# A two-block model on one core: x loaded first, side chains placed later, attention's end reordered

## The chip, the core and the metric

The kernel runs on one core of a Trainium2 chip, in one launch. The metric is the device time of that core in microseconds (us). Before the change the median of three runs is 2711.17 us (2707.82 to 2712.11). Engines go by short names: PE is TensorE (matmuls), DVE VectorE, ACT ScalarE, POOL GpSimd, SP the engine that issues all transfers.

## The reference, cut to what matters

512 tokens, width 1024, batch 1. Two blocks of two layers each run one after the other; all weights and activations are float32.

```
# first block, layer 0
mod = silu(c) @ ada_w + ada_b             # shift, scale, gate, twice per layer
h   = rmsnorm(x) * (1 + sc1) + sh1
u   = h @ pool_w_in                       # then trailing means over 2, 4, 8, 16 tokens
x  += g1 * (grouped(pooled) @ pool_w_out)
h   = rmsnorm(x) * (1 + sc2) + sh2
a, v = split(h @ ffn_w_up)                # 2 x 2816
x  += g2 * ((silu(causal_conv3(a)) * v) @ ffn_w_down)
# first block, layer 1: the pooling is replaced by attention
hkv = rmsnorm(x) * (1 + kv_sc) + kv_sh
q, kv = h @ w_q, hkv @ w_kv               # 3 branches (dilation 1, 4, 16) x 16 heads x 64
out_g, lse_g = banded_causal_softmax(q_g, k_g, v_g)
o   = sum_g softmax_g(lse) * out_g
x  += g1 * (o @ w_o)                      # then the same feed-forward
# second block, two layers
rq, rk, rv, rg, sq, sk, sv = split(rmsnorm(x) @ w_in)
ret = groupnorm(retention(rotary(rq), rotary(rk), rv)) * silu(rg)   # 4 heads x 128
sb  = headnorm(stick_breaking(sq, sk, sv))                          # 4 heads x 128
x  += concat(ret, sb) @ w_out
x  += (silu(h @ w_gate) * (h @ w_up)) @ w_down
# at each block's end a final rmsnorm
```

## The kernel before, in words

**Layout.** x lies transposed in eight tiles of 128 channels by 512 tokens. Every weight tile (128 x 128) and every activation tile is split into a high part in a rounded float32 format and a low part, the rest; `mm3` makes one product of three matmuls of 512 columns: high x high, high x low, low x high. Weights come as 434 units of eight tiles in the order of their use (`fetch`); ACT rounds a unit (`wh`), DVE or, for every second unit in attention, POOL subtracts (`wl`). PSUM has eight banks of one 128 x 512 accumulator each (`ps`); tiles named `s` are the 58 work tiles.

**Order of work.** A scheduler places each engine's instructions ahead of time, by the order of the program and by its own estimate of when inputs are ready; on the chip each engine then takes them in that order. The program's order is made by hand with a planner clock `pe["clk"]` (line 227 on): `mm3` adds 0.65 to it, and after each product `pump` looks at three streams. A stream holds generators; each `yield t` means "go on once the clock is t further" (counted from before the step). Stream 0 holds attention's branch cores and combinations and the stick-breaking heads, stream 1 the norms and retention heads, stream 2 the modulation vectors, whose rows (`araw`, 512 KB for 128 outputs) DVE multiplies with the condition and sums. In the first stage (`order["on"]`) DVE and ACT keep the program's order exactly.

**Start (`pool_mixer`, line 562).** The condition row is loaded first, then vectors and identity, the first scale and shift tiles (`AdaFirst`), the eight tiles of x, and so on. ACT squares x, DVE adds the squares, PE sums over channels (`mean`), a reciprocal root and a broadcast give R, and `prepare(m)` makes h for channel tile m.

**Norms (`norm_gen`, line 522).** The other norms of the first block run beside a first product on unnormalized input (`RawNorm`, `gemm_raw`, four output columns, 32 products): the mean is taken some planner time into it, 4.5 before a feed-forward and 2.5 before attention; 2.5 later comes the broadcast; then eight tiles are normalized, modulated and split. The shift's part of the raw product is accumulated on DVE from the raw weights (`shifted`) and summed over channels by PE behind the raw product (`shift_cols`). `Stat.add` squares on ACT and adds on POOL, for the last two tiles on DVE.

**Attention (line 951).** For each of four groups of four heads, `branch_qkv` makes q, k and v of three branches: the undilated one takes v transposed like q and k and turns it, the dilated ones take v directly (96 matmuls of 256 columns). Behind it the branch's core goes to stream 0 (`branch_core`, line 763): scores of a first pair of heads, 8 later their transposes and the scores of the second pair, 2 later the first values, 5 later the second transposes, 3 later the second values. After the third branch `combine` (line 889) weighs the three. At the end `out_proj` (line 984) runs once for each group: eight output columns of two products, each followed by an update of x on DVE (line 993).

**Retention (line 1089).** In each layer of the second block `mixer2` makes q and k of four heads, one product of eight steps each, turns them by the rotary tables (three DVE multiplications and one POOL addition, line 1165), and puts `ret_head` on stream 1: four score blocks at once, 3 later the outputs and their norm, 7 later transposes and gate. Behind it comes the output product: four columns at a time, first the four stick-breaking heads, then the four retention heads.

## Time and profile before

| | |
|---|---|
| median of three runs | 2711.17 us |
| the profiled execution | 2713.44 us |
| its span, first to last instruction | 2711.7 us, mean granted clock 0.993 |
| instructions | 32544, of them 12952 matmuls |
| PE, DVE, ACT, POOL busy | 98%, 52%, 38%, 12% of the span |
| transfers | 297.69 MB, 110 GB/s |

Rows come from one profiled execution. A group's row names line, engine, operation, output and inputs by the program's tile names, shapes and the count. "Idle before" is the time that the engine stood still before an instruction, with the engine whose work ended the wait. Times of a matmul overlap with the next; what one costs is the distance between starts. Line 140 is a wrapper through which all DVE and ACT instructions pass, so tile names tell them apart. The granted clock of PE has two levels, 0.50 (1.2 GHz) and 1.00 (2.4 GHz).

### The profile page before, as it was taken

The page shows a single profiled execution, that of the slowest core. Times are in us where ns is not written, and L with a number is a line of the kernel's source. Part 1 is how long each engine was busy: PE and PEld are TensorE (multiplying, and loading weights), DVE is VectorE, ACT ScalarE, POOL GpSimd, SP SyncE. Part 2 cuts the span into 40 slices and gives each one's busy share as a digit, 9 for nine tenths or more (in the row PEclk, how much of TensorE's full clock was granted, in tenths as well). Part 3 has the DMA queues.
Part 4 walks back from the last instruction along what each step waited for, and adds up shares of the span by engine and source line. Part 5 has one row for each costly group of instructions (what it writes and reads, how often), then busy time and mean ns, then how long its engine had stood idle before and what let it go on. Part 6 is the DMA issues. An engine that isn't in the chain of part 4 may idle for free.

```text
span 2711.7 us, 32544 instructions
## 1 busy us (share of the span) xinstructions
PE 2645.2 (98%) x12952; PEld 2184.3 (81%) x12952; DVE 1399.8 (52%) x2137; ACT 1029.9 (38%) x1720; POOL 320.0 (12%) x242
## 2 busy tenths in 40 slices
PE   6999999989999999999999999999999999999998
PEld 5878888778888888788888887888888887888887
DVE  7886566764333436753444456543434347543432
ACT  4453233544434344542344451422233451422233
POOL 0000000211221212000003011210111011110111
PEclk9999999999999999999999999999999999999999
DMA  8655555443222221222323211222233221223231
GB/s 317 230 163 179 171 178 169 144 157 116 71 77 72 78 68 66 93 101 93 101 94 117 78 62 63 93 94 101 93 101 117 80 69 47 101 93 101 94 101 47
DMA packets 86230, 297.69 MB, mean 110 GB/s; under 512 B 9574, under 2 KB 10302, under 8 KB 86078
## 3 DMA queue, kind: packets, MB, share of 16 engines
q1 hardware_dynamic: 86078, 295.61, 32.6%
q8 instruction: 101, 1.65, 0.3%
q14 instruction: 51, 0.42, 0.1%
HBM read 293.48 MB, written 2.10 MB: 109 GB/s over the span
## 4 chain that ended last, share of the span: by engine, by line
PE 61%; DVE 2%; POOL 1%; issue 0%; ACT 0%; DMA 0%; SPq 0%; DVEq 0%; POOLq 0%
PE ps L274 19%; PE ps L275 18%; PE ps L276 18%; PE ps L281 4%; DVE s L140 1%; PE ps L285 1%; POOL s L1165 0%; DVE x L140 0%; DVE wl L140 0%; ACT s L140 0%; PE ps L774 0%; PE ps L773 0%; PE ps L772 0%; PE ps L1071 0%; PE ps L1070 0%
## 5 line engine op out<-in xcount | busy, mean ns | idle before, releaser
L274 PE MATMUL ps<-s,wh 128*128 128x512 f32 x3152 | 1241.4, 395 | 0.2 <-DVE s L140 0.2
L275 PE MATMUL ps<-s,wh 128*128 128x512 f32 x3152 | 1232.2, 391 | 0.0
L276 PE MATMUL ps<-s,wl 128*128 128x512 f32 x3152 | 1230.8, 391 | 0.0
L140 ACT ACTIVATE wh<-raw 128x1024 fp32r<-128x1024 f32 x434 | 459.4, 1059 | 1024.1 <-PE ps L275 783.2
L140 DVE TENSOR_TENSOR wl<-raw,wh 128x1024 fp32r<-128x1024 f32 x394 | 492.2, 1249 | 494.5 <-ACT wh L140 482.7
L274 PEld LDWEIGHTS ps<-s,wh 128*128 128x128 f32 x3152 | 593.4, 188 | 129.6 <-issue 7.2
L276 PEld LDWEIGHTS ps<-s,wl 128*128 128x128 f32 x3152 | 593.2, 188 | 125.1 <-issue 1.1
L275 PEld LDWEIGHTS ps<-s,wh 128*128 128x128 f32 x3152 | 593.8, 188 | 119.6 <-DVE s L140 0.4
L140 ACT ACTIVATE s<-s 128x512 fp32r<-128x512 f32 (+6 forms) x288 | 167.9, 584 | 182.0 <-DVE s L140 118.6
L140 DVE TENSOR_TENSOR s<-s,s 128x512 fp32r<-128x512 f32 (+3 forms) x202 | 140.4, 698 | 75.6 <-ACT s L140 74.9
L431 POOL TENSOR_TENSOR s<-s,s 128x512 f32<-128x512 f32 x40 | 62.1, 1558 | 973.0 <-ACT s L140 972.5
L140 DVE TENSOR_TENSOR s<-ps,s 128x512 f32<-128x512 f32 (+6 forms) x164 | 103.8, 647 | 139.0 <-PE ps L276 128.8
L281 PE MATMUL ps<-s,s 128*64 128x128 f32 (+7 forms) x1376 | 156.9, 309 | 16.9 <-POOL s L1165 12.6
L140 DVE TENSOR_TENSOR s<-s,ps 128x512 f32<-128x512 f32 x108 | 73.1, 686 | 194.1 <-PE ps L276 168.2
L281 PEld LDWEIGHTS ps<-s,s 128*128 128x128 f32 (+2 forms) x1376 | 124.5, 174 | 55.3 <-issue 17.9
L211 POOL TENSOR_TENSOR wl<-raw,wh 128x1024 fp32r<-128x1024 f32 x40 | 99.8, 2494 | 414.4 <-ACT wh L140 368.5
L140 ACT ACTIVATE s<-ps 128x512 f32<-128x512 f32 (+5 forms) x188 | 97.0, 530 | 114.1 <-PE ps L281 66.9
L1198 POOL TENSOR_TENSOR s<-s,s 128x512 f32<-128x512 f32 x44 | 76.4, 1737 | 536.6 <-ACT s L140 536.6
L140 DVE COPY s<-ps 128x512 f32<-128x512 f32 (+2 forms) x73 | 48.7, 673 | 148.2 <-PE ps L285 77.1
L140 DVE SCALAR_TENSOR_TENSOR araw<-araw,cond 128x1024 f32<-128x1024 f32 x96 | 119.0, 1242 | 10.4 <-DMA araw<-in_adaw 10.4
L140 ACT ACTIVATE s<-s,st 128x128 f32<-128x128 f32 (+1 forms) x192 | 79.7, 417 | 52.3 <-DVE st L140 52.3
L140 ACT ACTIVATE s<-x 128x512 f32<-128x512 f32 x72 | 45.1, 626 | 95.2 <-DVE x L140 92.7
(117 smaller groups left out, 1770.7 us busy)
## 6 DMA issues: line engine op xcount, KB each, us to landing
raw<-in_wstream SPq DMA_DIRECT2D x434, 512.0 KB, 3.3
araw<-in_adaw SPq DMA_DIRECT2D x96, 512.0 KB, 4.3
s<-in_adaw SPq DMA_DIRECT2D x32, 256.0 KB, 6.0
x<-in_xT SPq DMA_DIRECT2D x8, 256.0 KB, 5.3
s<-in_dret SPq DMA_DIRECT2D x8, 256.0 KB, 4.5
out<-s SPq DMA_DIRECT2D x8, 256.0 KB, 2.6
s<-in_rope SPq DMA_DIRECT2D x4, 256.0 KB, 5.1
cond<-in_crow SPq DMA_DIRECT2D x1, 512.0 KB, 4.0
```

The source lines that it names most:

```text
L140: r = f(*a, **kw)
L211: (nc.gpsimd if u % 2 and st["spread"] else nc.vector).tensor_tensor(l, raw, h.bitcast(F32), op=ALU.subtract)
L274: nc.tensor.matmul(out, wH, xH, start=start, stop=False, **kw)
L275: nc.tensor.matmul(out, wH, xL, start=False, stop=False, **kw)
L276: nc.tensor.matmul(out, wL, xH, start=False, stop=stop, **kw)
L281: nc.tensor.matmul(out, lhsT, rhs, start=start, stop=stop, **kw)
L285: nc.tensor.transpose(out, in_, idn)
L431: eng.tensor_tensor(self.ss, self.ss, q, op=ALU.add)
L1198: nc.gpsimd.tensor_tensor(s, s, R, op=ALU.mult)
```

## The change

- The eight tiles of x are loaded right after the condition row, and each scale and shift column of the first norm is made one round later.
- The mean of a norm comes 8.5 planner us into the raw product (4.5 before), attention's 4.0 (2.5 before).
- `since` gives what is left of a time counted from a noted clock. An undilated core waits until 1.5 after its v is turned, a retention head until 4.0 after its k product.
- In the last branch of the last head group the core goes to its stream before the v product, makes both pairs of scores first, and waits for v before the values.
- The first two head groups of the output projection share one accumulator and one update of x per column; groups three and four follow.
- In the norm after attention the sums of squares are added on DVE for the last six tiles (two before).
- The wrapper of DVE and ACT is left out where it does nothing, so the profile shows those instructions at their own lines.

```diff
@@ -256,6 +258,10 @@
+    def since(clk, us):
+        return max(0.0, clk + us - pe["clk"])
     def pump():
@@ -520,7 +526,7 @@
     def norm_gen(stat, specs, out, residues):
-        yield 2.5 if residues else 4.5
+        yield 4.0 if residues else 8.5
         y = rstd(stat.mean())
@@ -565,14 +571,13 @@
         gs = cp.tile([P, KT], F32, name="gs0")
+        for m in range(KT):
+            nc.sync.dma_start(x[m], xT[m])
         nc.sync.dma_start(vec, vecs)
...
             sh.load(m)
-            if m == 0:
-                for i in range(KT):
-                    nc.sync.dma_start(x[i], xT[i])
             fetch()
@@ -590,20 +595,19 @@
                 wh = issue_high()
-            if m + 2 < KT:
-                columns(m + 2)
+            if m + 1 < KT:
+                columns(m + 1)
             h.append((hm, low(t, hm)))
...
-        columns(0)
         for m in range(KT):
...
         o = stat.mean()
-        scale_column(1)
+        scale_column(0)
         y = rstd(o)
         wh = issue_high()
-        sh.column(1)
+        sh.column(0)
         R = bcast(y)
@@ -726,8 +730,10 @@
-    def branch_qkv(hg, br, h, hkv, pre=()):
+    def branch_qkv(hg, br, h, hkv, pre, core):
         d = ORDER[br]
+        early = hg == 3 and br == 2
         col = br * D + hg * 256
@@ -753,6 +759,9 @@
                 k.append(t)
+        v = []
+        if early:
+            core(q, k, v)
         ov = [ps(), ps()]
@@ -774,14 +783,14 @@
                     pump()
-        v = []
         for i in range(2):
...
             v.append(t)
-        return q, k, v
-    def branch_core(hg, br, q, k, v, parts):
+        if not early:
+            core(q, k, v)
+    def branch_core(hg, br, q, k, v, parts, begun, last):
@@ -873,11 +882,17 @@
         N = []
+        if d == 1:
+            yield since(begun, 1.5)
         first = scores(0)
+        second = scores(1) if last else None
         yield Y[0]
         first = turn(first)
-        second = scores(1)
-        yield Y[10]
+        if not last:
+            second = scores(1)
+        yield 1.0 if last else Y[10]
+        while not v:
+            yield 0.5
         N.append(values(0, first))
@@ -967,33 +982,41 @@
         nx2 = nx2()
-        stat = nx2
         for hg in range(4):
             for br in range(3):
-                q, k, v = branch_qkv(hg, br, h, hkv, pre[2 * br:2 * br + 2] if hg == 0 else ())
-                streams[0].add(branch_core(hg, br, q, k, v, parts))
-                if br == 2:
-                    streams[0].add(combine(parts, done))
-        out_proj(0, done, g1, stat)
-        out_proj(1, done, g1, stat)
-        out_proj(2, done, g1, stat)
-        drain(streams[0])
-        out_proj(3, done, g1, stat)
-        return nx2
-    def out_proj(hg, done, g1, stat):
-        while len(done) <= hg:
-            pe["clk"] = max(pe["clk"], streams[0].ready)
-            streams[0].step()
+                def core(q, k, v):
+                    streams[0].add(branch_core(hg, br, q, k, v, parts, pe["clk"], hg == 3 and br == 2))
+                    if br == 2:
+                        streams[0].add(combine(parts, done))
+                branch_qkv(hg, br, h, hkv, pre[2 * br:2 * br + 2] if hg == 0 else (), core)
         g1 = g1()
-        for m in range(KT):
-            o = gemm([("attn_w_o", (0,), 256 * hg, m * P)], done[hg], range(2))[0]
+        def heads(hg):
+            while len(done) <= hg:
+                pe["clk"] = max(pe["clk"], streams[0].ready)
+                streams[0].step()
+            return done[hg]
+        def part(o, m, hg, start, stop):
+            for kt in range(2):
+                wH, wL = wt("attn_w_o", (0,), 256 * hg + kt * P, m * P)
+                mm3(o, wH, wL, *heads(hg)[kt], start and kt == 0, stop and kt == 1)
+        def put(o, m):
             xv = x[m].rearrange("p (i r) -> p i r", r=4)
...
                                            op0=ALU.mult, op1=ALU.add)
-            if hg == 3:
-                stat.add(m)
-        done[hg] = None
+        for hgs in ((0, 1), (2,), (3,)):
+            for m in range(KT):
+                o = ps()
+                for hg in hgs:
+                    part(o, m, hg, hg == hgs[0], hg == hgs[-1])
+                put(o, m)
+                if hgs[-1] == 3:
+                    nx2.add(m)
+        return nx2
@@ -1086,8 +1109,9 @@
-    def ret_head(l, h, q, k, v, sgs, dec, out):
+    def ret_head(l, h, q, k, v, sgs, dec, out, begun):
         a = []
+        yield since(begun, 4.0)
         for j in range(NB):
@@ -1169,7 +1193,7 @@
             k = rotary(gemm([col("rk", hd)], h, range(KT))[0])
-            streams[1].add(ret_head(l, hd, q, k, rv, sgs, dec, ret))
+            streams[1].add(ret_head(l, hd, q, k, rv, sgs, dec, ret, pe["clk"]))
         while len(sb) < 4:
@@ -1255,7 +1279,7 @@
     nx = box["nx"]
-    nx = attention(nx, (nx.gs, mods[(1, 0)]), (gk, mods[("kv", 0)]), mod((1, 2)), next_norm("norm2_g", 1, (1, 4)))
+    nx = attention(nx, (nx.gs, mods[(1, 0)]), (gk, mods[("kv", 0)]), mod((1, 2)), next_norm("norm2_g", 1, (1, 4), 6))
     if stop == 3:
```

## Rows read from the trace of the kernel before

**Rows 1.** The page: busy time, share of the span and instructions of the engines.

```profile
PE 2645.2 (98%) x12952; PEld 2184.3 (81%) x12952; DVE 1399.8 (52%) x2137; ACT 1029.9 (38%) x1720; POOL 320.0 (12%) x242
```

**Rows 2.** Waits of PE: who waited for whom, us in total, times, longest.

```profile
PE ps L281 <- DVE s L140: 30.8, 9, 16.1
PE ps L281 <- POOL s L1165: 12.6, 8, 2.8
PE ps L285 <- ACT s L140: 7.0, 9, 2.1
...
PE ps L285 <- DVE cc L140: 0.8, 1, 0.8
```

**Rows 3.** Stretches: length; busy time (instructions) per engine; granted clock, DMA share, GB/s.

```profile
2.00:14.00 12.00, 0.00 (x0) 0.00 (x0) 6.10 (x16) 6.84 (x10) 0.00 (x0) 1.00 1.01 362
527.90:531.30 3.40, 3.40 (x9) 2.65 (x9) 3.40 (x5) 1.31 (x2) 0.00 (x0) 0.50 0.90 301
579.10:585.90 6.80, 6.00 (x39) 4.32 (x39) 6.20 (x11) 3.60 (x12) 0.00 (x0) 0.50 0.49 163
1094.60:1101.30 6.70, 6.70 (x19) 5.35 (x19) 5.64 (x12) 0.41 (x2) 0.00 (x0) 0.50 0.52 165
1668.00:1674.80 6.80, 5.91 (x12) 3.81 (x13) 1.90 (x4) 0.00 (x0) 0.83 (x1) 0.50 0.00 0
```

**Rows 4.** Timeline, undilated scores of the second group: start, us, instruction [idle before].

```profile
682.39 0.40 PE L275 MATMUL ps<-s,wh 128*128 128x512 f32 x1
682.62 0.40 PE L276 MATMUL ps<-s,wl 128*128 128x512 f32 x1
...
683.55 1.28 DVE L140 COPY s<-ps 128x512 f32<-128x512 f32 x2
...
684.28 1.79 PE L281 MATMUL ps<-s,s 64*128 64x128 f32 x16 [1.26 <-DVE s L140]
```

**Rows 5.** Timeline of PE, retention scores of the second and fourth heads.

```profile
1633.62 2.87 PE L281 MATMUL ps<-s,s 128*128 128x512 f32 x12 [1.55 <-POOL s L1165]
...
1668.89 4.64 PE L281 MATMUL ps<-s,s 128*128 128x512 f32 x8 [2.82 <-POOL s L1165]
```

**Rows 6.** Timeline, the start.

```profile
5.96 1.28 ACT L140 ACT_TABLE_LOAD   x1
...
9.28 5.36 ACT L140 ACTIVATE s<-x 128x512 f32<-128x512 f32 x8 [2.04 <-DMA x<-in_xT]
...
10.61 5.47 DVE L140 TENSOR_TENSOR s<-s,s 128x512 f32<-128x512 f32 x7 [0.90 <-ACT s L140]
...
16.14 1.86 PE L281 MATMUL ps<-one,s 128*128 128x1 f32 x8 [16.14 <-DVE s L140]
...
24.96 0.80 PE L274 MATMUL ps<-wh,s 128*128 128x512 f32 x1 [3.36 <-ACT s L140]
```

**Rows 7.** Timeline, first feed-forward's norm: mean, and last low part.

```profile
142.50 1.05 PE L281 MATMUL ps<-one,s 128*128 128x1 f32 x8 [2.24 <-DVE s L140]
...
173.66 0.69 DVE L140 TENSOR_TENSOR s<-s,s 128x512 fp32r<-128x512 f32 x1 [1.59 <-ACT s L140]
```

**Rows 8.** Timeline, attention's norm: broadcast, last shift accumulation, its sum.

```profile
507.87 1.16 PE L281 MATMUL ps<-ct,rsy 128*128 128x128 f32 x8 [1.27 <-DVE rsy L140]
...
525.22 0.74 DVE L140 SCALAR_TENSOR_TENSOR s<-raw,mod,s 128x512 f32<-128x512 f32 x1
...
526.01 1.05 PE L281 MATMUL ps<-one,s 128*128 128x1 f32 x8 [3.35 <-DVE s L140]
```

**Rows 9.** Timeline, end of attention: splits, POOL's additions, mean.

```profile
1083.05 1.57 DVE L140 SCALAR_TENSOR_TENSOR s<-x,gain,s 128x512 fp32r<-128x512 f32 x1
...
1084.04 6.83 POOL L431 TENSOR_TENSOR s<-s,s 128x512 f32<-128x512 f32 x4
...
1092.47 0.74 DVE L140 SCALAR_TENSOR_TENSOR s<-x,gain,s 128x512 fp32r<-128x512 f32 x1
...
1093.96 1.33 PE L281 MATMUL ps<-one,s 128*128 128x1 f32 x8 [4.51 <-DVE s L140]
```

More of the change, by code (lines that the diff above doesn't have):

```diff
@@ L137, in __getattr__ @@
             f = getattr(self.engine, name)
+            if not order["on"]:
+                return f
             def call(*a, **kw):
                 r = f(*a, **kw)
-                return tc.keep_in_program_order(r) if order["on"] else r
+                return tc.keep_in_program_order(r)
             return call
```

## The prediction

> **What bounds the kernel now.** I read the page's busy line first: TensorE (PE) is busy 2645.2 of 2711.7 us [rows 1]. Its matmuls can't get fewer here (the change removes none), so only two things can give time back: moments in which PE waits, and stretches in which it runs at its lower clock. Next the list of PE's waits [rows 2]: 30.8 us for VectorE (DVE) in nine places, 12.6 us for a GpSimd (POOL) addition of line 1165 in eight, 7.0 us for ScalarE (ACT) in nine. Then the windows: after some of these waits the granted clock reads 0.50 for 3.4 to 6.8 us [rows 3], which is 1.2 instead of 2.4 GHz, so about half of each such window is lost on top of the wait. Last, the timeline around each wait, to see what PE had behind the waiting matmul. PE takes its matmuls in order: a matmul that waits holds back whatever stands behind it, even if that is ready. Most waits here are of this kind: a small matmul of a side chain stands too early in PE's order and ready products stand behind it. One product of three matmuls costs 0.69 us (starts 0.23 apart, [rows 4]); I call it a step. The code moves side chains by planner time (0.65 a step), and looks only at the end of a step.
>
> **The change part by part.** Gains are against the profiled execution.
>
> *Retention scores later (`ret_head` waits until 4.0 after its product).* Now the first scores stand behind one step and wait for the rotary's POOL addition: 1.55 us for the second head of a layer (the third is alike, the first shorter), 2.82 for the fourth [rows 5], 12.6 us over the eight heads of both layers [rows 2]. After the fourth, 6.8 us pass at clock 0.50 [rows 3], half of it lost; the second layer repeats this, so 6.8 us for both. Later means the seventh step instead of the first: six steps, 4.1 us, more than the longest wait. What fills it is the next head's product, for the fourth head the output product of the stick-breaking heads, whose weights and inputs are there. Behind the fourth head's scores the planner gives 3 and 7 us until its transposes: with the 4.1 and some 2 of evacuation 16 us, and its result is asked for after 28 steps (19 us), so it stays covered; if it weren't, PE would wait that rest at the output product's last head. Bounds: 10 (the waits halved, clock falls kept in one layer) to 19.4 (12.6 + 6.8). Taken, nearest to the rows: **18.5**.
>
> *Undilated scores later (1.5).* Three groups of four show the same picture: after one step the scores wait 1.26 us for two copies on DVE that stand behind the last split of the combination before [rows 4]. Later means the third step: 1.38 us. Each wait is just covered, with a tenth to spare. Bounds 2 (one of three stays, half of another) to 4.5 (also 0.2 us that each restart costs). Taken **3.9**.
>
> *Start.* ACT loads its table until 7.24 us, but the first square of x starts at 9.28, because x is queued behind two constant tables and four 256 KB tiles; the eight squares run 0.67 apart, seven additions on DVE follow from 1.33 us later, then the mean (16.14) and the first product (24.96) [rows 6]. With x queued right behind the 512 KB condition row, 2.6 MB at the 362 GB/s of this stretch [rows 3] are 7.2 us: the first x lands near 5.6 and the last near 10.5 (estimate from that rate and from the condition row being in at 4.9), ahead of its square (7.24 + 7 x 0.67 = 11.9). So the squares start at 7.24, and everything up to the first product 2.0 us earlier. The passed loads (vectors, identity, the first scale and shift tiles) land 5.4 us later, about 14 at the latest; they are first used once the additions are done, at 14.0, and each later column's tiles are used one round later than now. The raw weight tile keeps its place. Bounds 1 to 2.3 at this place.
>
> *Means of the norms later (4.5 to 8.5, 2.5 to 4.0).* The mean moves from the eighth step to the fifteenth (in attention from the fifth to the eighth): up to 4.8 (2.1) us. First feed-forward: PE waits 2.24 us for the sum of squares [rows 7]. That goes, as PE has weights and split inputs for its raw product. But what is late next is visible in the same group: from this mean runs a chain (reciprocal root, broadcast, then eight times multiply, two scalings, subtract) whose last low part ends at 174.35, 31.9 us after the mean. PE finishes its raw product before that and then lives on what the chain delivers. PE leaves for the mean at 140.26 now; with the sum ready at 142.45 the mean comes between there and 145.1, and the chain's end moves with it by 0 to +2.6 us, unless the three shift accumulations that now stand inside the chain come ahead of it (0.66 each, -2.0). Also, it is DVE that PE waits for here, so the 2.0 us of the start may arrive at this sum as a wait again. Start and this norm together: bounds -1 to 4.2, taken **2.0**.
>
> Attention's norm: the broadcast waits 1.27 us and the shift's column sum 3.35, since the last accumulation stands at 525.22 behind the eight normalizations; 3.4 us at clock 0.50 follow [rows 3, 8], so at most 1.27 + 3.35 + 1.7 = 6.3. With the mean 2.1 us later that accumulation should come ahead of the normalizations, but these, and the split inputs that PE needs next, come up to 2 us later. Bounds -2 to 6.3; taken **2.5**. The ACT waits in the first group (7.0 us [rows 2], and 6.8 us at 0.50 [rows 3]) stand in a stretch in which DVE is busy 6.20 of 6.80 us; moving the first scores by two steps shortens a part of them. Bounds -3 to 4, taken **1.0**.
>
> *End of attention.* PE waits 4.51 us for the last sum of squares, and 6.7 us at clock 0.50 follow [rows 3, 9]: 7.9 us; a wait in the last combination is 0.8 [rows 2]. The mean's seven steps (4.8 us) alone cover 4.51. DVE's queue also gets shorter: sharing accumulators for the first two head groups takes out eight updates of x (0.66 us each from start to start, 5.3 us); four additions move from POOL to DVE (+2.4 us), and the five splits that took 1.12 to 1.57 us beside POOL's additions should take 0.74 again [rows 9] (-2.4). The scores of the last branch go ahead of its 96 value matmuls, so that softmax and transposes run beside these; the last combination starts some 10 us earlier and finishes well before the third group's product is through. What it adds: the first values come right behind the value product and may wait up to 0.9 us for two copies on ACT (0.6 each); the second scores may wait up to 1.4 us for the copy of their key, at the front of PE's queue with the value product behind. As in the first feed-forward, the chain behind the mean then limits: some 2 us of the 7.9 stay. Bounds 3 to 8.7 (7.9 + 0.8); taken **6.5**.
>
> Sum: 18.5 + 3.9 + 2.0 + 2.5 + 1.0 + 6.5 = **34.4 us**. The profiled execution took 2713.44 us (span 2711.7), so 2679.0; the median of the three runs is 2.3 us below the profiled one, 2711.17, so the forecast is 2711.2 - 34.4 = **2677 us**, 1.3% less.
>
> **Rivals.**
> - *The norm chains are the bound* (late means starve PE). For it: PE has no slack at 174.35 [rows 7]. Then start and first norm give 0, attention's -2, the end 3, the rest as above: 0 - 2 + 1 + 3 + 3.9 + 18.5 = 24.4, 2687 us. Against it: the first group's products can be taken in another order while one is late.
> - *Everything is covered*: 4 + 6.3 + 3 + 4.4 + 8.7 + 19.4 = 45.8, 2665 us.
> - *The retention delay does nothing*: four equal bubbles per layer could mean that accumulators are short and not that the order is bad. Each score needs a bank of eight, the running product one, and the next tile is only taken when one is free. Then the waits stay, and the time is 2677 + 18.5 = 2695 us. Against it: the waits end with POOL's addition, not with a bank's release [rows 5].
>   The Trainium skill ("Perfetto Trace Analysis", Optimization Strategy) says that the same gap repeating on the engine that should be saturated can mean too little SBUF or PSUM for the next tile. By that rule the time would be this rival's 2695; the releaser in the row speaks against it.
> - *Slower*: the delayed scores take four banks while the output product of four columns holds the other four. Where DVE frees them late, PE stops in the middle, and the clock falls for each head, not for one of four: per head 3.5 us of wait and 3.4 of clock, 8 x 6.9 = 55, against the 19.4 of now: +36, less the 15.9 of the other parts, 2731 us. It decides from 4.4 us a head. Against it: those scores need four banks now too, and no wait beside the eight for line 1165 stands at them [rows 2, 5].
>
> **How the numbers follow.** Forecast 0.60 (its own range 2668 to 2686), norm chains 0.17, everything covered 0.12, retention unchanged 0.06, slower 0.03, all parts cancelling 0.02. A measurement of this kernel tells 0.2% (5.4 us) from no change. Faster: 0.60 + 0.17 + 0.12 + 0.06 = 0.95; same 0.02; slower 0.03. The range takes in the forecast, the norm chains and nearly all of the covered case: 2662 to 2692.
>
> **What would show it.** In the profile after: no wait of PE for line 1165 and no clock of 0.50 after the fourth retention head; no wait of the undilated scores; the first square at 7.2 us and the first product near 23; no 4.5 us wait at the end of attention; PE still waiting in attention's first group. I am wrong if POOL still releases PE's retention scores, if new waits for split inputs stand behind the three norms, or if clock 0.50 shows up in new places.

## The result, and the profile after

The changed kernel takes 2681.9 us (median of 4 runs, 2679.2 to 2683.1) against 2710.7 for the kernel before, run beside it: a ratio of 0.9894, 95% interval 0.9877 to 0.9911, or 28.8 us less. The forecast was 2677 with a range of 2662 to 2692. The direction and the size hold; one term of the sum, the largest, was 6 us too large, and the mechanism given for it was not the one that worked.

The page after, its busy line (compare [rows 1]): PE has the same 12952 matmuls and is busy 9 us less. Up to its last matmul the granted clock reads 0.50 for 30.7 us in the profile before and for 10.2 us in this one; half of the difference, 10 us, accounts for that.

```profile
PE 2636.0 (98%) x12952; PEld 2180.2 (81%) x12952; DVE 1390.0 (52%) x2133; ACT 1028.5 (38%) x1720; POOL 314.0 (12%) x238
```

PE's waits after (columns as in [rows 2]; L142 and L471 are VectorE lines, L1189 is POOL's addition, L1165 before):

```profile
PE ps L287 <- DVE s L142: 14.4, 1, 14.4
PE ps L287 <- DVE rsy L471: 4.5, 3, 2.0
PE ps L287 <- POOL s L1189: 3.6, 4, 1.4
...
PE ps L291 <- ACT s L838: 3.0, 4, 1.6
PE ps L287 <- DVE s L760: 1.9, 1, 1.9
...
PE ps L281 <- DVE s L521: 1.2, 2, 0.8
```

Without the one long wait of the start, the waits for VectorE are down from 18.9 to 10.4 us (all its entries of either list), POOL's from 12.6 to 3.6, but not to nothing. The broadcasts of three more norms than the start's wait for the reciprocal root (rsy), where only attention's did, and two products for the low part of a normalized input (L521).

Three places of the timeline after: undilated scores without their wait [rows 4], the two low parts at attention's norm [rows 8], and the broadcast at the end of attention, the only wait left at that norm [rows 9].

```profile
524.59 0.50 PE L281 MATMUL ps<-s,wh 128*128 128x512 f32 x1 [0.45 <-DVE s L521]
...
526.34 0.61 PE L281 MATMUL ps<-s,wh 128*128 128x512 f32 x1 [0.77 <-DVE s L521]
...
681.52 1.79 PE L287 MATMUL ps<-s,s 64*128 64x128 f32 x16
...
1093.19 1.13 PE L287 MATMUL ps<-ct,rsy 128*128 128x128 f32 x8 [0.94 <-DVE rsy L471]
```

Stretches after (columns as in [rows 3]):

```profile
2.00:14.00 12.00, 0.00 (x0) 0.00 (x0) 4.49 (x7) 6.70 (x11) 0.00 (x0) 1.00 1.02 354
151.10:154.50 3.40, 3.40 (x11) 2.72 (x10) 1.99 (x3) 1.69 (x3) 0.00 (x0) 0.50 0.83 329
526.60:530.00 3.40, 3.40 (x9) 2.61 (x9) 3.40 (x7) 3.40 (x6) 0.00 (x0) 0.50 0.94 355
557.30:560.70 3.40, 3.40 (x17) 2.34 (x15) 2.92 (x5) 0.00 (x0) 0.00 (x0) 0.50 0.86 274
1091.00:1095.00 4.00, 3.06 (x18) 2.42 (x17) 2.69 (x7) 0.00 (x0) 0.00 (x0) 1.00 0.88 308
1651.00:1658.00 7.00, 7.00 (x43) 6.21 (x42) 4.40 (x19) 1.47 (x3) 0.00 (x0) 1.00 0.23 75
```

The clock stays at 1.00 at the end of attention and behind the fourth retention head (the last two rows). As long as PE has work it reads 0.50 three times, each time behind a wait: at the first feed-forward's norm, where it was 1.00 in the profile before, at attention's norm, and in the first group. The first of these places isn't new: in ten executions with that norm as before, the clock falls there in seven.

**Time by stretch.** The landmarks are the starts of the nth matmul on PE in the trace. Eleven kernels of this study differ from the kernel before in one part only, so for every stretch there are 7 to 12 executions that hold this stretch as it was before; their mean and spread stand beside the one value of the kernel after. The last column is the forecast.

```
stretch (matmul n to m)           as before: mean (spread), n       after    gain   forecast
to the first matmul               16.25 (16.04 to 16.48), 11        14.40    1.85  |
0 to 480                          109.31 (108.62 to 109.95), 11     109.65  -0.34  | 2.0
480 to 720, first norm            56.37 (54.09 to 58.13), 10        56.03    0.34  |
720 to 2200                       335.33 (335.26 to 335.46), 12     335.51  -0.18
2200 to 2310, attention's norm    29.95 (29.24 to 30.63), 11        27.43    2.52    2.5
2310 to 2600, first group         52.15 (51.53 to 52.79), 10        51.21    0.94    1.0
2600 to 5200, undilated scores    407.00 (406.95 to 407.05), 11     403.05   3.95    3.9
5200 to 5900, end of attention    139.88 (138.97 to 140.61), 7      132.53   7.35    6.5
7900 to 8500, retention, layer 1  131.20 (130.27 to 133.13), 8      125.44   5.76  | 18.5
10700 to 11400, the same, layer 2 152.54 (150.98 to 153.83), 8      146.15   6.39  |
the other three stretches         each the same within 0.1 in all executions, but for one value 0.3 above the rest
```

The gains add up to 28.7 us (with 0.1 of the other three), and 28.8 were measured; that they meet so closely is partly chance, as the one execution after is the slowest of its four (2683.1 us, median 2681.9). The spread is itself a result: against the one profile before, the first norm would seem to lose 1.6 us (54.39 to 56.03), because this execution had its clock up there, and retention would seem to gain 15.4.

### The profile page after: what moved, and what is told of

Read it like the earlier page. It is cut to its first block, busy times and chain, and to the rows that moved or that the text cites. A ratio compares the mean times of both kernels' runs of the same rounds, so it can differ in the third digit from the quotient of the medians.

```text
span 2681.4 us, 32545 instructions
## 1 busy us (share of the span) xinstructions
PE 2636.0 (98%) x12952; PEld 2180.2 (81%) x12952; DVE 1390.0 (52%) x2133; ACT 1028.5 (38%) x1720; POOL 314.0 (12%) x238
## 4 chain that ended last, share of the span: by engine, by line
PE 91%; DVE 5%; DMA 1%; ACT 1%; issue 1%; POOL 0%; DVEq 0%; POOLq 0%; ACTq 0%
PE ps L280 27%; PE ps L282 26%; PE ps L281 26%; PE ps L287 6%; PE ps L291 1%; DMA araw<-in_adaw 1%; PE ps L781 1%; PE ps L783 1%; PE ps L782 1%; DVE araw L373 1%; DVE s L336 1%; DVE wl L213 0%; DVE s L437 0%; DVE s L506 0%; POOL s L1189 0%
## 5 line engine op out<-in xcount | busy, mean ns | idle before, releaser
L208 ACT ACTIVATE wh<-raw 128x1024 fp32r<-128x1024 f32 x426 | 450.9, 1059 | 1020.8 <-PE ps L281 781.0
L213 DVE TENSOR_TENSOR wl<-raw,wh 128x1024 fp32r<-128x1024 f32 x386 | 477.7, 1238 | 485.6 <-ACT wh L208 476.0
L437 POOL TENSOR_TENSOR s<-s,s 128x512 f32<-128x512 f32 x36 | 55.5, 1548 | 969.0 <-ACT s L435 968.7
L287 PEld LDWEIGHTS ps<-s,s 128*128 128x128 f32 (+2 forms) x1376 | 121.9, 172 | 42.0 <-issue 15.4
L1222 POOL TENSOR_TENSOR s<-s,s 128x512 f32<-128x512 f32 x44 | 76.3, 1734 | 536.7 <-ACT s L456 536.7
L1224 DVE TENSOR_TENSOR s<-s,ps 128x512 f32<-128x512 f32 x44 | 30.3, 688 | 140.6 <-PE ps L282 128.1
L456 ACT ACTIVATE s<-s 128x512 f32<-128x512 f32 x96 | 59.6, 624 | 102.0 <-DVE s L706 85.8
L351 ACT ACTIVATE s<-s 128x512 fp32r<-128x512 f32 x104 | 65.5, 630 | 70.7 <-POOL s L959 42.6
L352 DVE TENSOR_TENSOR s<-s,s 128x512 fp32r<-128x512 f32 x104 | 71.4, 686 | 30.2 <-ACT s L351 30.2
L1219 DVE TENSOR_TENSOR s<-ps,s 128x512 f32<-128x512 f32 x44 | 30.4, 691 | 106.4 <-PE ps L282 106.4
L280 PE MATMUL ps<-wh,s 128*128 128x512 f32 x192 | 78.0, 406 | 3.4 <-ACT s L142 3.4
L281 PE MATMUL ps<-wl,s 128*128 128x512 f32 x192 | 76.2, 397 | 0.0
```

The source lines that it names most:

```text
L208: nc.scalar.activation(h, raw, AF.Copy)
L213: (nc.gpsimd if u % 2 and st["spread"] else nc.vector).tensor_tensor(l, raw, h.bitcast(F32), op=ALU.subtract)
L280: nc.tensor.matmul(out, wH, xH, start=start, stop=False, **kw)
L281: nc.tensor.matmul(out, wH, xL, start=False, stop=False, **kw)
L287: nc.tensor.matmul(out, lhsT, rhs, start=start, stop=stop, **kw)
L351: nc.scalar.activation(h, src, AF.Copy)
```

## The experiments

**Theories.** A is the prediction's: a delay moves a step later in PE's order, behind what it waits for. B came from the trace after. In the kernel after the retention scores stand 18 or 24 product matmuls behind their key's product, in the kernel before 24 (18 at the fourth head). So they stood eight steps (six at the fourth head) behind it all along. I put that down to the scheduler, which takes the planner's order and places the scores where it reckons their inputs ready; the delay of 2.0 below, which leaves three heads where they were, bears this out. What moved is VectorE's queue. The timeline before, at the second head of layer 1 (start, us, instruction, idle before):

```profile
1627.04 0.75 DVE L140 SCALAR_TENSOR_TENSOR s<-ps,vec,s 128x512 f32<-128x512 f32 x1
1627.15 1.30 POOL L1165 TENSOR_TENSOR s<-s,s 128x512 f32<-128x512 f32 x1 [11.46 <-DVE s L140]
1627.71 1.82 DVE L140 TENSOR_TENSOR wl<-raw,wh 128x1024 fp32r<-128x1024 f32 x1
...
1629.45 0.68 DVE L140 TENSOR_TENSOR s<-s,s 128x512 fp32r<-128x512 f32 x1
1630.06 2.08 DVE L140 TENSOR_TENSOR s<-ps,s 128x512 f32<-128x512 f32 x3
1632.30 1.26 POOL L1165 TENSOR_TENSOR s<-s,s 128x512 f32<-128x512 f32 x1 [3.86 <-DVE s L140]
```

The key's product has ended near 1626, but its rotary (1630.06, three operations) stands behind the previous head's gate scaling, a weight's low part and that head's low part. The same place after:

```profile
1611.06 0.69 DVE L1185 TENSOR_TENSOR s<-ps,s 128x512 f32<-128x512 f32 x1 [0.61 <-PE ps L282]
...
1613.18 1.23 DVE L213 TENSOR_TENSOR wl<-raw,wh 128x1024 fp32r<-128x1024 f32 x1
1613.30 2.27 POOL L1189 TENSOR_TENSOR s<-s,s 128x512 f32<-128x512 f32 x1 [5.68 <-DVE s L1188]
1614.33 0.75 DVE L1127 SCALAR_TENSOR_TENSOR s<-ps,vec,s 128x512 f32<-128x512 f32 x1
```

The rotary (its first operation is shown) waits for PE alone, and the old head's tail comes behind it. PE's scores after (all four heads of a layer; the third still has the tail ahead of it):

```profile
1600.88 2.42 PE L287 MATMUL ps<-s,s 128*128 128x512 f32 x8 [0.43 <-POOL s L1189]
...
1615.62 2.42 PE L287 MATMUL ps<-s,s 128*128 128x512 f32 x8
...
1634.41 2.42 PE L287 MATMUL ps<-s,s 128*128 128x512 f32 x8 [1.39 <-POOL s L1189]
...
1649.17 2.42 PE L287 MATMUL ps<-s,s 128*128 128x512 f32 x8
```

**The retention delay alone.**

```diff
 def ret_head(l, h, q, k, v, sgs, dec, out, begun):
+    yield since(begun, 4.0)
```

> The kernel before with one part of the change alone: the retention head's scores are issued only 4.0 planner microseconds after its product. Theory A (the prediction's): the delay puts the scores six steps later in PE's order, behind POOL's addition; then no wait of PE for that addition is left in either layer and the gain is 18.5 us (10 to 19.4). Theory B (formed from the trace of the changed kernel): the scores' place in PE's order hardly moves (18 or 24 product matmuls after the key's product, 24 before); what moves is the tail of the previous head, three VectorE operations (scaling by the gate, the low weights of a raw tile, the low part) that stood ahead of the next key's rotary in VectorE's queue. They are gone from there for the second and the fourth head and not for the third. Then waits of some 0.4 us (first head) and 1.4 us (third) stay in each layer, no clock of 0.50 follows the fourth head, and the gain is 15.8 us, what the change gave in the two retention stretches, within 1.5.

2700.2 us against 2710.5, ratio 0.9958 (0.9944 to 0.9973): 10.3 us. The waits left are those that B names, four of 0.40 to 1.39 us, 3.5 in all. Against its profile of before the gain is 15.4 us in the two stretches; against the mean of eight executions it is 12.2; the timed interval, 7.3 to 15.2 us, holds the second of these. So B names the waits, but its 15.8 us is missed as A's 18.5 is: both numbers were read against that one profile.

**The delay at 2.0.**

```diff
-    yield since(begun, 4.0)
+    yield since(begun, 2.0)
```

> The kernel before with the delay of the retention scores at 2.0 instead of 4.0, nothing else. Theory A: two microseconds of delay are three steps, 2.07 us; that is more than the waits of the second and third heads (1.55) and leaves 0.75 of the fourth's 2.82, so of 19.4 us at most 2 x 0.75 of waits stay, and perhaps the clock's fall behind them: gain 11 to 18 us. Theory B: in this kernel the three operations of the previous head's tail still stand ahead of the next key's rotary on VectorE for the second, third and fourth heads, and the scores still stand 24 to 26 product matmuls behind the key's product; so the waits stay as they are, and the gain is 0 to 2 us.

2706.4 us, ratio 0.9984 (0.9975 to 0.9994): 4.1 us; the two stretches gain 6.0. The second and third heads wait 1.58 and 1.55 us as before, as B says, and the first 0.40. But the fourth waits 1.11 instead of 2.82, with the clock up: its scores stand 26 instead of 18 product matmuls behind. So for three heads a delay doesn't move the scores, for the fourth it does. A and B each miss a part.

**The delay of 4.0 with the old end of the head.**

```diff
-Y = [8, 2, 4, 0.2, 3, 11, 4, 6, 3, 7, 2, 5, 3, 1.5]
+Y = [8, 2, 4, 0.2, 3, 11, 4, 6, 3, 3, 2, 5, 3, 1.5]
```

> The kernel before with the retention scores delayed by 4.0, and the pause ahead of a head's transposes shortened from 7 to 3, so that the head's end comes at the planner time that it has in the kernel before. Theory A: the scores are as late as in the change, so the gain is as large, about 16 to 18.5 us. Theory B: with the end of the head back at its old time the three operations of its tail are ahead of the next key's rotary again, for three heads of four in each layer, with the head's normalization just before them; the waits for POOL's addition stay for those heads and may be longer (the scores stand 23 product matmuls behind the key's product): gain at most 2 us, or a loss of up to 8.

2702.7 us, ratio 0.9969 (0.9957 to 0.998): 7.8 us, in the two stretches 9.4. B's number is wrong. The tail stands ahead of the rotary again for three heads of four, but the waits there are 0.84 to 0.89 us:

```profile
1627.20 0.75 DVE L140 SCALAR_TENSOR_TENSOR s<-ps,vec,s 128x512 f32<-128x512 f32 x1 [0.86 <-PE ps L288]
1628.18 1.22 DVE L140 TENSOR_TENSOR wl<-raw,wh 128x1024 fp32r<-128x1024 f32 x1 [0.23 <-ACT wh L140]
1629.33 0.68 DVE L140 TENSOR_TENSOR s<-s,s 128x512 fp32r<-128x512 f32 x1
1629.93 2.09 DVE L140 TENSOR_TENSOR s<-ps,s 128x512 f32<-128x512 f32 x3
1632.16 1.27 POOL L1169 TENSOR_TENSOR s<-s,s 128x512 f32<-128x512 f32 x1 [8.62 <-DVE s L140]
...
1633.49 1.45 PE L284 MATMUL ps<-s,s 128*128 128x512 f32 x3 [0.84 <-POOL s L1169]
```

The low part of the weight takes 1.22 us here and 1.82 before, where POOL adds the query's rotary beside it. What counts is when the tail is done, and its rank in the queue only as far as it sets that. I keep B in this form: the wait is the end of the key's rotary (3.5 to 4.5 us from its first operation to the end of POOL's) less the time at which PE reaches the scores, and both can be moved.

**The delay at 7.0.**

```diff
-    yield since(begun, 4.0)
+    yield since(begun, 7.0)
```

> The kernel before with the retention scores delayed by 7.0, nothing else. Now no head has the previous head's tail ahead of its key's rotary, and the scores of all eight heads stand 33 product matmuls (7.6 us) behind the key's product. Theories A and B agree that all eight waits for POOL's addition go, with the clock's fall behind the fourth heads: 12.6 + 6.8 = 19.4 us. Theory C: the heads' results become late instead; the fourth head ends some 17 us after its product, and the output product asks for it after 28 steps (19 us), so if its normalization takes longer than planned PE waits there; then a wait of one or more us at the output product's last head appears in each layer, and the gain stays at or below that of the delay of 4.0 (15.8).

2696.2 us, ratio 0.9946 (0.9929 to 0.9963): 14.3 us; the two stretches gain 17.2. All eight waits for POOL are gone, and no new one stands at the output product, so C is out; the 19.4 of A and B is 2 us too much, again by the clock (see below). The second head of layer 1: POOL is done at 1629.89, and the scores come 1.2 us later.

```profile
1627.63 2.26 POOL L1169 TENSOR_TENSOR s<-s,s 128x512 f32<-128x512 f32 x1 [9.66 <-DVE s L140]
...
1631.10 2.32 PE L284 MATMUL ps<-s,s 128*128 128x512 f32 x8
```

**The undilated scores alone.**

```diff
+        if d == 1:
+            yield since(begun, 1.5)
         first = scores(0)
```

> The kernel before with the undilated branch's first scores 1.5 later, nothing else. Theory A (the prediction's): the waits of 1.26 us in the second to fourth groups go, 3.9 us (2 to 4.5), and about 1 us more from the first group's waits for ScalarE. Theory B: the first group's waits have another cause (VectorE is full there) and don't move, or move to a later matmul; then 3.9 us and nothing in the first group.

2708.4 us, ratio 0.9991 (0.9982 to 1.0), which tells little; the stretch tells more. Matmuls 2600 to 5200 take 403.04 us against 406.95 to 407.05 in eleven other executions: 3.96. The first group takes 49.96, below all ten others (51.53 to 52.79): 2.2 us. But its waits for ScalarE are not shorter, as A has it: they are 7.0 us as in [rows 2] (line L288 here, L285 there), and all waits of PE in this stretch are 7.5 us against 6.7 to 7.8 in the ten others, which is B's mechanism. What is different is the clock: in the ten others 3.4 or 6.8 us of this stretch read 0.50, in this execution none. Whether the delay keeps the clock up there or chance does, one execution can't show. This execution also shows a fourth retention head that waits as long as in [rows 5] and loses no clock behind it: the window of the first layer reads 1.00 where [rows 3] has 0.50. In its second layer 3.4 us at 0.50 follow the same wait.

```profile
PE ps L288 <- ACT s L140: 7.0, 8, 2.3
```

```profile
1664.88 2.42 PE L284 MATMUL ps<-s,s 128*128 128x512 f32 x8 [2.81 <-POOL s L1170]
```

```profile
1663.00:1671.00 8.00, 6.12 (x36) 5.02 (x37) 2.23 (x6) 0.00 (x0) 1.26 (x1) 1.00 0.04 16
```

**The start alone.**

```diff
+        for m in range(KT):
+            nc.sync.dma_start(x[m], xT[m])
         nc.sync.dma_start(vec, vecs)
...
-            if m + 2 < KT:
-                columns(m + 2)
+            if m + 1 < KT:
+                columns(m + 1)
```

> The kernel before with x loaded first and the modulation columns made one round later, nothing else. Theory A (the prediction's): the first product comes 2.0 us earlier (1 to 2.3; the changed kernel showed 1.7) and the gain reaches the end: 1 to 2 us. Theory B: at the first feed-forward's norm it is VectorE that PE waits for, and what VectorE does until there doesn't end earlier, so the sum of squares is waited for some 1.7 us longer than the 1.9 to 3.6 us that five executions of the kernel before and of the retention variants show there: gain 0 at the end, and the first product 1.7 us earlier all the same.

2708.2 us, ratio 0.9991 (0.9982 to 1.0). The first matmul comes at 14.19 instead of 16.25, 2.06 earlier. The first norm's stretch then takes 57.90 us, and ten executions without this edit take 54.09 to 58.13, so this one value decides nothing; 6.8 us of it are at the low clock. The wait for the sum of squares is 2.95 us, inside the 1.9 to 3.6 us of the others and not 1.7 us longer, which speaks against B's mechanism. The median is 2.9 us lower: A by that too, but the interval reaches to no gain, so B's number isn't excluded.

**The later means alone.**

```diff
-        yield 2.5 if residues else 4.5
+        yield 4.0 if residues else 8.5
```

> The kernel before with the means of the two raw norms later (8.5 instead of 4.5, 4.0 instead of 2.5), nothing else. Theory A (the prediction's): at the first feed-forward's norm the wait for the sum (1.9 to 3.6 us in five executions, the longer ones with a clock of 0.50 behind them) goes, of which 0 to 4 us arrive; attention's norm gives 2.5 (-2 to 6.3): together 2.5 to 5 us. Theory B (the rival of the norm chains): the chain from the mean on is the bound; the broadcast waits for the reciprocal root in its place, as the changed kernel shows (2.0 us and a clock of 0.50), and what is gained at the sum is lost there: first norm 0, attention's norm 0 to 2, together at most 2.

2706.0 us, ratio 0.998 (0.9971 to 0.999): 5.1 us. Attention's norm takes 25.87 us instead of 29.95, which is A; in part it is the clock, which stays up in this execution and reads 0.50 for 3.4 or 6.8 us in the eleven others. At the two other norms B's mechanism is seen: the sum is no longer waited for, the broadcast is, 1.98 us at the first feed-forward and 4.03 at the end of attention.

```profile
1099.66 1.75 PE L281 MATMUL ps<-ct,rsy 128*128 128x128 f32 x7 [4.03 <-DVE rsy L140]
```

These two stretches take 55.81 us (0.6 less than the mean as before) and 138.45 us (1.4 less).

**The end of attention alone**, and then without each of its three parts.

```diff
+        early = hg == 3 and br == 2
...
+        for hgs in ((0, 1), (2,), (3,)):
...
-next_norm("norm2_g", 1, (1, 4))
+next_norm("norm2_g", 1, (1, 4), 6)
```

> The kernel before with the end of attention alone: the last branch's scores ahead of its values, the first two head groups' output products in one accumulator, and the mean behind it at the seventh step. Theory A (the prediction's): the 4.5 us wait for the last sum of squares and the clock's fall behind it go, less 2 us for the chain behind the mean: 6.5 us (3 to 8.7). Theory B (formed from the trace of the changed kernel, where the landmarks gave 7.7): the chain behind the mean costs only 0.9 us, the wait of its broadcast, so 7.9 + 0.8 - 0.9 = 7.8 us. Theory C (the rival of the norm chains): 3 us.

2706.6 us, ratio 0.9986 (0.9976 to 0.9995): 4.5 us; the stretch takes 134.84 instead of 139.88, 5.0 us: between the numbers of A and C, within A's bounds, and not B's. The wait for the sum shrinks from 4.51 to 1.53 us; 3.4 us at clock 0.50 still follow (3.4 or 6.8 where this part is as before). The kernel after takes 132.53 there, 2.3 less, with the later mean beside this part (alone it gave 1.4); of these 2.3 us, 1.7 are the clock, which stays up.

```diff
-        for hgs in ((0, 1), (2,), (3,)):
+        for hgs in ((0,), (1,), (2,), (3,)):
```

> The end of attention alone (as in the run before it) without the shared accumulators: the first and second head groups each add their output product to x again, so VectorE has eight more updates of x. In the kernel before PE waits 4.51 us for the last sum of squares, with the end of attention alone 1.53. Theory A (the prediction's): the shorter queue of VectorE is a part of the gain; with eight updates of 0.66 more (5.3 us) the wait for the sum goes back to 3 us or more. Theory B: these updates lie in stretches in which VectorE has time, before the third group's product is through; then the wait stays at 1.2 to 1.9 us and the time is that of the end of attention alone.

2707.4 us, the stretch 139.99: nothing of the 5.0 us is left in this execution. The wait for the sum is 1.53 as B says, but A's price is paid at another place, in the last combination, whose small operations stand on VectorE between the eight updates:

```profile
1056.81 0.60 PE L291 MATMUL ps<-ct,cc 128*12 128x128 f32 x4 [1.19 <-DVE cc L939]
1058.85 1.65 PE L954 MATMUL ps<-s,selr 44*128 44x512 f32 x3 [1.45 <-DVE s L947]
```

```profile
1058.10:1064.90 6.80, 6.05 (x14) 4.33 (x15) 3.31 (x5) 1.57 (x2) 3.31 (x3) 0.50 0.00 0
```

With shared accumulators PE waits only 0.29 us there. Of the 5.15 us, 3.4 are the low clock behind these waits. This execution is the slowest of its ten (2714.7 us), and the medians of the two kernels are only 0.8 us apart, so what sharing is worth on most executions is not shown.

```diff
-next_norm("norm2_g", 1, (1, 4), 6)
+next_norm("norm2_g", 1, (1, 4))
```

> The end of attention alone with five of the seven additions to the sum of squares on POOL again (as in the kernel before) instead of one. Theory A: POOL's additions stretch the splits on VectorE beside them (1.12 to 1.57 us against 0.74) and each takes longer than on VectorE, so the last sum comes later: the wait for it is 2.5 us or more, against 1.53. Theory B: the last two additions are on VectorE in both, and what precedes them is the last product's update and split; then the wait stays at 1.5 within 0.4.

2709.0 us, the stretch 137.43, 2.6 more. The wait for the sum is 2.49, and 6.8 us at clock 0.50 follow instead of 3.4, which makes 1.7 of the 2.6: A, at the edge of its number.

```diff
-        early = hg == 3 and br == 2
+        early = False
```

> The end of attention alone without the early scores: the last branch's scores follow its values again, one pair after the other. Theory A (the prediction's): the last combination then starts some 10 us later; its wait of 0.8 us for the combination's weights comes back, and the third group's product (11 us) no longer covers all of it, so 1 to 3 us are lost against the end of attention alone. Theory B: the combination is done in time in either order; only the 0.8 us wait comes back, and the wait for the sum stays 1.5.

2709.0 us, the stretch 137.72, 2.9 more. The combination waits 0.52 and 0.43 us again, which both theories have, but the wait for the sum is 3.54, which neither had; I take it that the late combination pushes what VectorE does for the last products, and did not test this by itself. In time this is A's 1 to 3 us. The three medians lie within 2.4 us of that of the whole part and their intervals overlap with it, so the split rests on one profile each.

**A version that beats both.** The kernel after with two numbers changed:

```diff
-    yield since(begun, 4.0)
+    yield since(begun, 7.0)
...
         y = rstd(stat.mean())
-        yield 2.5
+        yield 2.5 if residues else 7.0
```

> The changed kernel with two numbers of its planner changed: retention scores delayed by 7.0 instead of 4.0, and the broadcast of the reciprocal root, in the two norms without residues, 7.0 instead of 2.5 after its mean, which puts it some seven product matmuls (1.6 us) later in PE's order. Theory A: the four waits for POOL's addition that the change left (3.6 us) go, and the broadcast's waits (2.0 us with a clock of 0.50 behind it in the first feed-forward, 0.9 at the end of attention) shrink to at most 0.5 and the clock stays up: 3.6 + 2.4 + 1.7 = 7.7 us less than the change's 2681.9, so 2674. Theory B: in the norms VectorE's chain behind the broadcast is the bound, and what PE no longer waits at the broadcast it waits at the first modulated input: only the retention's 3.6 to 4 us, 2678. Theory C: the fourth retention head comes too late for the output product: no gain, 2682.

2676.2 us (2674.7 to 2676.7), ratio to the kernel before 0.9878 (0.9863 to 0.9893), 5.8 us less than the change. Retention gives 5.0 of that (122.92 + 143.66 us), the first norm 1.4 (its broadcast waits 0.24, and its clock stays up). At the end of attention 1.2 are lost, which is B: the broadcast (first row) waits for nothing now, and three low parts of the next inputs are waited for behind it (0.23, 0.48 and 0.46 us). The same three waits are new at the first norm (0.24, 0.48 and 0.46 us), so B's mechanism is there too, and what is gained goes with the clock. In this execution attention's norm, which the edit leaves alone, had its clock up (25.90, 1.5 less).

```profile
1091.15 1.05 PE L287 MATMUL ps<-ct,rsy 128*128 128x128 f32 x8
...
1102.95 0.50 PE L281 MATMUL ps<-s,wh 128*128 128x512 f32 x1 [0.23 <-DVE s L521]
1105.84 0.50 PE L281 MATMUL ps<-s,wh 128*128 128x512 f32 x1 [0.48 <-DVE s L521]
```

## Why the prediction was right, and where it was not

The total came inside the range because the five other terms each came within 1 us of what was measured, and the largest, though its mechanism was wrong, still gave two thirds of its number. That it gave so much by another route is luck.

**Retention scores, 18.5 forecast, 12.2 measured.** Two steps failed.

- "The first scores stand behind one step", and a delay makes that seven. They stood behind eight already (six at the fourth head), which the order of the instructions shows and the timeline of PE would have shown by counting. The delay of 4.0 moved the head's tail out of the way for two heads of four; 3.6 us of waits stayed. At 7.0 they go, and the stretches gain 5.0 more. The sentence "no wait of PE for line 1165" in the list of what would show it is refuted, and with it the first sign of being wrong came: POOL still releases PE's scores.
- "6.8 us for both" layers, for the clock. That was read from one execution. In the eight executions with retention as before, each with two fourth heads that wait 2.8 us, 6.8 us at clock 0.50 follow twice, 3.4 us nine times and nothing five times: 2.8 us on average, of which half is lost, 1.4, so 2.8 us for both layers instead of 6.8. Together with the waits that is 12.6 + 2.8 = 15.4, and 17.2 is what the delay of 7.0 gave (the remainder, 0.2 for each restart, was left out of the sum).

The rival of retention unchanged is refuted as to its cause: the delay of 7.0 removes all eight gaps with the same buffers. Too little SBUF or PSUM, which the Trainium skill ("Perfetto Trace Analysis", Optimization Strategy) gives as a possible meaning of a repeating gap, is not the cause here: the releaser in the rows is POOL's addition, and the gaps end with it.

**Start and first norm, 2.0 forecast, 1.7 measured** (1.85 - 0.34 + 0.34 - 0.18). The first square starts at 7.70, when the table load ends, and the first product at 23.24, as forecast within 0.5 us:

```profile
6.40 1.28 ACT L142 ACT_TABLE_LOAD   x1
...
7.70 4.27 ACT L142 ACTIVATE s<-x 128x512 f32<-128x512 f32 x8
...
14.40 1.87 PE L287 MATMUL ps<-one,s 128*128 128x1 f32 x8 [14.40 <-DVE s L142]
...
23.24 0.80 PE L280 MATMUL ps<-wh,s 128*128 128x512 f32 x1 [3.37 <-ACT s L142]
```

The later mean gave next to nothing, as the bounds of start and norm together (-1 to 4.2) allowed, but by a link that I had not named. Not the last low part of the chain is late; the broadcast is, at once:

```profile
141.80 1.05 PE L287 MATMUL ps<-one,s 128*128 128x1 f32 x8
142.31 1.23 DVE L213 TENSOR_TENSOR wl<-raw,wh 128x1024 fp32r<-128x1024 f32 x1
143.45 2.33 DVE L336 SCALAR_TENSOR_TENSOR s<-raw,mod,s 128x512 f32<-128x512 f32 x3
145.69 0.15 DVE L477 TENSOR_SCALAR var<-ps 128x4 f32<-128x4 f32 x1
...
150.00 0.16 DVE L471 TENSOR_TENSOR rsy<-rsy,rsb 128x4 f32<-128x4 f32 x1
...
150.21 1.28 PE L287 MATMUL ps<-ct,rsy 128*128 128x128 f32 x8 [2.03 <-DVE rsy L471]
```

The mean is done by 142.85, and VectorE takes it up at 145.69, behind a weight's low part and three shift accumulations; five short operations then take until 150.16 among more of the same.

**Attention's norm, 2.5 and 2.5.** The shift's column sum is no longer waited for (3.35 us). The broadcast still is, 1.53 us against 1.27, and two low parts are new (0.45 and 0.77 us, with 3.4 us at 0.50 behind): the sign of new waits for split inputs came at this norm and not at the other two. Alone the part gave 4.1, with the clock up.

**First group, 1.0 and 0.9.** A number from wide bounds that met by luck. The step behind it, that later scores shorten the waits for ScalarE, failed: with that delay alone they stayed at 7.0 us. In the kernel after they are 4.7, but 2.5 us are waited for VectorE instead of 0.5, 7.2 in all against 6.7 to 7.8 before. What was gained goes with the clock: 3.4 us at 0.50 here, 6.8 in seven of the ten executions as before and 3.4 in three.

**Undilated scores, 3.9 and 3.95.** Right in mechanism and size.

**End of attention, 6.5 and 7.35.** The wait of 4.51 us and the clock's fall are gone. That fall, taken as 6.7 us from one execution, is 6.8 in four of the seven executions as before and 3.4 in three, so that term was about 0.7 us too large. The chain behind the mean costs 0.94 us at the broadcast instead of the 2 set aside. That the shorter queue of VectorE matters is borne out by one profile, without shared accumulators; that it works through the last combination was not said.

**The rivals.** The norm chains are no bound for the kernel, yet their mechanism is there at two norms when the mean alone is moved. The slower case did not come: in both retention stretches PE waits for POOL's addition alone, not for a bank.

## What to carry to other kernels

A wait on an in-order engine is a difference of two times: when the producer is done, and when the consumer is reached. Before pricing a delay, count what already stands between, and look at what stands ahead of the producer in its own queue. Moving one link of a chain later uncovers the next one, so move the links together. And what depends on the clock is priced from several executions, stretch by stretch, never from one.

## What the runs showed of the hardware

- The same wait before the same matmuls (2.8 us at the fourth head) was followed by 0, 3.4 or 6.8 us at the lower clock (1.2 GHz) in different executions. Of the waits up to 1.6 us at retention scores, none was followed by a fall.
- VectorE and POOL hold each other up. The low part of a weight (128x1024, two inputs) took 1.82 us where POOL's addition had begun 0.56 us before it and 1.22 without; the addition took 2.27 us where that operation had begun 0.12 us before it, and 1.26 without. The Trainium skill ("SBUF — State Buffer", SBUF: two separate sides) says that the two share a pair of ports, that of a VectorE operation with two inputs in SBUF and a POOL operation that reads SBUF the first to start holds it for its whole instruction, and that the other stands still. By that the two would take 1.96 and 2.37 us, an estimate (the rest of the other's time, 0.74 and 1.11, on top); the trace agrees within 0.15.
